# Splitting the value products of two attentions into one sum, and moving the first raw MLP weights

## The chip, the cores and the metric

The kernel runs on one core of one Trainium2 chip. A core has several engines that work side by side, each through its own instructions in order: TensorE (PE) multiplies matrices, with its weight loads shown apart as PEld; VectorE (DVE) and ScalarE (ACT) do elementwise work and read what TensorE left in PSUM; GpSimd (POOL) does some elementwise work; SyncE (SP) issues most of the DMA transfers. Data lies in HBM, in SBUF (128 partitions) and in PSUM, where matmuls accumulate. Engines wait for one another through semaphores.

The metric is the device time of one execution in microseconds (us). The kernel before took 1761.11 us, the median of three runs (1760.59 to 1767.72).

## What is computed

One layer of a decoder trunk on 1024 tokens of width 1024, in float32:

```python
h = rms_norm(x, pre_mix_g[l])
proj = h @ w_in[l]
...
oa = diff_attention(qa, ka, va, lam)
oa = rms_norm(oa, diff_head_g[l]) * (1.0 - lam_init)
ya = oa.reshape(b, s, A_WIDTH) @ w_a_out[l]
...
for g, (window, dil) in enumerate(B_PAIRS):
    o_g, lse_g = dilated_group(qb[:, :, g], kb[:, :, g], vb[:, :, g], window, dil)
...
yb = ob.reshape(b, s, B_WIDTH) @ w_b_out[l]
g_a, g_b = jnp.split(jax.nn.sigmoid(gates), 2, axis=-1)
mix = (g_a * ya + g_b * yb) @ w_mix_out[l]
x = x + rms_norm(mix, post_mix_g[l])
h = rms_norm(x, pre_ffn_g[l])
u = causal_depthwise_conv(h @ w_up[l], conv_w[l], conv_b[l])
gate, val = jnp.split(u, 2, axis=-1)
y = (jax.nn.gelu(gate, approximate=True) * val) @ w_down[l]
x = x + rms_norm(y, post_ffn_g[l])
```

Attention A has 4 heads with two score maps each (softmax one minus lambda times softmax two, then times the values). Attention B has three groups of 4 heads, each a band of a strided subsequence. In both, the last step is a product of probabilities and values, and that step is one of the two places of the change. The other is the loading of `w_up`, the first weights of the MLP.

## The kernel before

**Split operands.** A float32 number is kept as two tiles of a type that TensorE multiplies fast, `hi` and `lo`: ACT copies the number into `hi` (L143) and VectorE subtracts that from it into `lo` (L140). This is `split`. A full product is three matmuls, hi x hi, hi x lo and lo x hi, that accumulate in one PSUM bank (`mm3`, L147 to L149).

**Stages, in order.** Projections and attention A, with projections of the next heads and of gates as filling between attention steps; attention B, filled the same way (about 80 to 925 us); branch A (`ya`) and branch B, each a product with an output matrix, times a gate; the mixing product row by row (`mix_row`, L989 to L991) with two normalizations and transposes (L980); the MLP in 22 blocks of 128 columns per half; the down product. Within the MLP the first three blocks (`full`) take 16 x 3 matmuls per unit; the others (`seven`) use a scheme with seven products of half size instead of eight, on sums of weights (`weights`) and sums of activations (t1 to t4).

**Value products.** `turned` transposes a block of probabilities on TensorE and splits it, so that a block `t` holds hi and lo side by side. `pv` multiplies the value block `vh` (the stationary operand) by hi and lo of `t` in one matmul (L484), into two separate sums that lie side by side in one bank, and `vl` by the hi part alone (L486) into the first sum. A use with two query blocks has 512 columns in L484 and 256 in L486, a use with one has 256 and 128. At the end of a group ACT copies the first sum into `osb` (L580 in attention A, L771 in B), and VectorE adds the second sum to it (L581, L772). The pool `ps_o` of these sums has one buffer.

**Branch B and its memory.** `ob`, the split operands of branch B, is a pool `mid_b` on the left side of SBUF, closed when branch B is issued. For each half of each of its 8 rows VectorE multiplies by the gate (L959), POOL adds `ya` (L960), and `split` writes `mh` and `ml`, which the mixing product reads. Weights of the mixing product are loaded and split in between. The pool `res` is opened after this on the left side, where `mid_b` was: it holds rows of `x`, normalized rows and gains.

**Raw weights.** `load_raw` (L120) loads half a weight unit (256 KB) by SyncE into the pool on top of the list `raws_in`. From branch B on this is `raw`, with five buffers, shared by the weights of branch B, of the mixing product and of the MLP. `slot_w` gives a pair of tiles for hi and lo from `wpool`, six buffers each. The two units of MLP block 0 are made by `up`, started as `first_ups` between the last mixing rows.

**From full to seven-product blocks.** `weights(f)` loads four raw halves a11, a12, a21, a22, splits a11 into `wpool` and a12 into `wb` and so on in turn, and makes the sums s1 to s4 (L1144). For the first such block this is called after the pools `wb` and `mid` have been opened in the memory of the sums t1 to t4, and after the last splits of these (the list `pieces`).

**Order.** The program is written in stages, but the order of the instructions on each engine is set when the program is built, by a planner that simulates a timeline; `tc.high_priority` moves some of them ahead. So an edit in one stage can change the order elsewhere.

Of the kernel before, what the change touches and what calls it, by code (L numbers as in the profile page):

```python
# [24 lines left out]
P = 128  # L25
# [18 lines left out]
FULL = 3  # L44
# [44 lines left out]
def trunk(ctx: ExitStack, tc: tile.TileContext, a, out):  # L89
# [18 lines left out]
    def psum(dt=F32, pool=acc, tag="acc"):  # L108
        return pool.tile([P, 512], dt, tag=tag, name=tag)
# [64 lines left out]
    def halves():  # L174
        return [slice(i * 512, (i + 1) * 512) for i in range(2)]
# [302 lines left out]
    def pv(o, vs, uses, hh, first, last):  # L478

        c = slice(hh * P, (hh + 1) * P)
        for n, (b, q0, q1, t) in enumerate(uses):
            nc.tensor.matmul(o[:, :, q0 : q1 + 1], vs[b // 4][0][:, b % 4, c], t, start=first and n == 0, stop=False)  # L484
        for n, (b, q0, q1, t) in enumerate(reversed(uses), 1):
            nc.tensor.matmul(o[:, 0, q0 : q1 + 1], vs[b // 4][1][:, b % 4, c], t[:, 0], start=False,  # L486
                             stop=last and n == len(uses))


# [30 lines left out]
    def attend_a(h, i, ops, vs, out_sb, pair):  # L520

        q0, q1, k0, k1, l0, l1 = ops
        scale = QK ** -0.5
        if i // 4 not in out_sb:
            out_sb[i // 4] = (wk_a.tile([P, 512], F32, tag="osb", name="osb", bufs=2),
                              tiny.tile([P, 4], F32, tag="eps4", name="eps4", bufs=2))
        osb, eps4 = out_sb[i // 4]
        qs = slice(i * P, (i + 1) * P)
        w = (i + 1) * P
        chunks = [(c, min(w, c + 512)) for c in range(0, w, 512)]  # L530
        mx = tiny.tile([P, 2, 2], F32, tag="mx", name="mx")
        sc = []
        for c, (qq, kk, ll) in enumerate(((q0, k0, l0), (q1, k1, l1))):
            s_sb = wk_a.tile([P, S], F32, tag="s", name="s", bufs=4)
            sc.append(s_sb)
            for n, (c0, c1) in enumerate(chunks):
                ps = psum(F32, ps_s, "s")[:, : c1 - c0]
                nc.tensor.matmul(ps, qq[:, qs], kk[:, c0:c1], start=True, stop=False)
                nc.tensor.matmul(ps, qq[:, qs], ll[:, c0:c1], start=False, stop=True)
                mask = mask_a[:, 512 - (c1 - c0) :] if c1 == w else mask_a[:, 0:1].to_broadcast([P, 512])  # L540
                nc.vector.tensor_tensor_reduce(
                    out=s_sb[:, c0:c1], in0=ps, in1=mask, scale=1.0, scalar=-3.0e38,
                    op0=ALU.add, op1=ALU.max, accum_out=mx[:, c, n : n + 1])
        if len(chunks) == 2:
            nc.vector.tensor_tensor(mx[:, :, 0], mx[:, :, 0], mx[:, :, 1], op=ALU.max)
        negm = tiny.tile([P, 2], F32, tag="negm", name="negm")
        nc.vector.tensor_scalar(negm, mx[:, :, 0], -scale, None, op0=ALU.mult)
        den = tiny.tile([P, 2], F32, tag="den", name="den")
        for c in range(2):
            nc.scalar.activation(sc[c][:, :w], sc[c][:, :w], AF.Exp, bias=negm[:, c : c + 1], scale=scale,  # L550
                                 accum_out=den[:, c : c + 1])
        rc = tiny.tile([P, 1], F32, tag="rc", name="rc")
        nc.vector.reciprocal(rc, den[:, 1:2])
        ratio = tiny.tile([P, 1], F32, tag="ratio", name="ratio")
        nc.vector.scalar_tensor_tensor(ratio, rc, den[:, 0:1], nlam, op0=ALU.mult, op1=ALU.mult)
        nc.vector.scalar_tensor_tensor(sc[0][:, :w], sc[1][:, :w], ratio, sc[0][:, :w], op0=ALU.mult, op1=ALU.add)

        nc.vector.scalar_tensor_tensor(eps4[:, i % 4 : i % 4 + 1], den[:, 0:1], EPS, den[:, 0:1], op0=ALU.mult, op1=ALU.mult)

        pair.append(sc[0])  # L560
        if i % 2 == 0:
            return
        two, po, ts = list(pair), [], {}
        pair.clear()
        groups = [[(b, n) for b in (2 * g, 2 * g + 1) for n in range(2) if b < i or n] for g in range((i + 1) // 2)]

        def turn(g):
            t = turned([two[n][:, b * P : (b + 1) * P] for b, n in groups[g]], wk_a, 3)
            for b in {b for b, _ in groups[g]}:
                at = [x for x, (bb, _) in enumerate(groups[g]) if bb == b]  # L570
                ts[b] = t[:, :, at[0] : at[-1] + 1]

        def add(b):
            if b == 0:
                po.append(psum(F32, ps_o, "o").rearrange("p (t n q) -> p t n q", n=2, t=2))
            uses = [(b, 0, 1, ts[b])] + ([(i, 1, 1, ts[i])] if b == i - 1 else [])
            pv(po[0], vs, uses, h % 2, b == 0, b == i - 1)
            if b == i - 1:
                o = osb[:, (i % 4 - 1) * P : (i % 4 + 1) * P].rearrange("p (n q) -> p n q", n=2)
                nc.scalar.activation(o, po[0][:, 0], AF.Copy)  # L580
                nc.vector.tensor_tensor(o, po[0][:, 1], o, op=ALU.add)  # L581
                if i % 4 == 1:
                    head_norm(h, i // 4, osb, eps4)

        def do(*todo):
            def fn():
                for f, x in todo:
                    f(x)
            return fn

        n = len(groups)
        later(1, do(*[(turn, g) for g in range(min(n, 2))]))
        if n > 2:
# [117 lines left out]
    def attend_b(g, h, jj, ops, vs, sbs):  # L711
# [46 lines left out]
                n += len(bs)  # L758

        def values():  # L760
            po = psum(F32, ps_o, "o").rearrange("p (t j q) -> p t j q", j=2, t=2)
            for us in [uses] if shared else [[us] for us in uses]:
                pv(po, vs, us, h % 2, True, True)
            hi, lo = po[:, 0], po[:, 1]
            if g == 0:
                to = osb[:, 2 * jj * P : 2 * (jj + 1) * P].rearrange("d (j q) -> d j q", j=2)
            elif g == 1:
                to = osb.rearrange("d (j q r) -> d r j q", r=4, j=2)[:, jj]
            else:
                to = osb.rearrange("d (i r) -> d r i", r=8)[:, 2 * jj : 2 * jj + 2]  # L770
            nc.scalar.activation(to, hi, AF.Copy)  # L771
            nc.vector.tensor_tensor(to, lo, to, op=ALU.add)  # L772
            if jj == 3:
                store_b(g, h, osb, stat)

# [173 lines left out]
    with st2:  # L949
# [88 lines left out]
        def up(f, part):  # L1038
# [3 lines left out]
            for half, sl in enumerate(halves()):  # L1042
# [4 lines left out]
                nc.scalar.activation(uu[:, 2 + half * 512 : 2 + (half + 1) * 512], ps, AF.Copy)  # L1047
                yield uu

        first_ups = [up(0, part) for part in range(2)]  # L1050
        for g in first_ups:
            next(g)
            turn_h2.pop(0)()
        assert not turn_h2


# [54 lines left out]
        return to  # L1111

    cv = open_pool(st_up, "cv", side="right")
    with ExitStack() as st_s:
        sums = open_pool(st_s, "sums")
        full(0)
        new_sum("t1", b12, b11)
        new_sum("t3", b22, b12, nc.gpsimd)
        full(1)
        new_sum("t2", b22, tt["t1"])  # L1120
        new_sum("t4", b21, tt["t2"])
        t3, t2, t4 = (split_sum(n) for n in ("t3", "t2", "t4"))
        for f in range(2, FULL):
            full(f)

        t1 = split_sum("t1", b12)
        while pieces:
            pieces.pop(0)()
# [1 line left out]
    wb = open_pool(st_up, "wb")  # L1130
    mid = open_pool(st_up, "mid")

    def weights(f):

        a11, a12, a21, a22 = (load_raw(a["w_up"][2 * f + part][:, sl]) for part in range(2) for sl in halves())
        ws = {}

        def put(name, src):
            ws[name] = slot_w(wb if len(ws) % 2 else None)
            split(*ws[name], src)  # L1140

        def combined(name, x, y, op):
            t = mid.tile([P, 512], F32, tag="s", name=name, bufs=4)
            nc.vector.tensor_tensor(t, x, y, op=op)  # L1144
            return t

        put("a11", a11)
        put("a12", a12)
        s1 = combined("s1", a21, a22, ALU.add)
        s2 = combined("s2", s1, a11, ALU.subtract)  # L1150
        put("s2", s2)
        put("s3", combined("s3", a11, a21, ALU.subtract))
        put("s1", s1)
        put("s4", combined("s4", a12, s2, ALU.subtract))
        put("a22", a22)
        return ws
# [47 lines left out]
            split(*operands[step][-1], src)  # L1204

    places = iter([lambda: slot_w(early, 2), slot_w] * 2 + [slot_w] * 4)
    ws = weights(FULL)
    for f in range(FULL, NF):
        if f + 1 == NF:
            for i in range(AHEAD):  # L1210
# [258 lines left out]
```

## Time and profile before

| what | us |
|---|---|
| median of three runs | 1761.11 |
| the profiled execution's own time | 1762.05 |
| span of its trace, first to last instruction | 1760.3 |

The profile is of one execution. In its rows an instruction group has a line, an engine, an operation and the tiles (`out<-in`); a wait has the engine that waits and the one that released it. Matmuls overlap in TensorE's pipeline, so the duration of one is longer than the distance to the next. The clock column is the share of full speed that TensorE was granted.

### The profile page before, as it was taken

Reading aid. Unit: us, or ns where it says so; the run is one execution under the profiler, and the core shown is the slowest. Engines: PE = TensorE matmul, PEld = TensorE weight load, DVE = VectorE, ACT = ScalarE, POOL = GpSimd, SP = SyncE. Lnnn points to the kernel's source line nnn. Section 1 sums busy time; section 2 is a strip of 40 time slices with the busy share of each in tenths; the row PEclk is TensorE's granted clock in tenths of the full one; section 3 lists DMA queues with packets and bytes.
Section 4 is the critical chain, followed back from the end, with each engine's and each line's share of the span. In section 5 each row is a group of like instructions: output and inputs, shape, how many; then the busy total and the mean of one; then the engine's idle time right before and its main releaser. Section 6 shows DMA issues by size and latency. Waiting matters only on the chain.

```text
span 1760.3 us, 24112 instructions
## 1 busy us (share of the span) xinstructions
PE 1717.8 (98%) x8754; PEld 1455.4 (83%) x8754; DVE 1327.4 (75%) x2612; ACT 867.7 (49%) x1585; POOL 51.6 (3%) x78
## 2 busy tenths in 40 slices
PE   9999999999999999999998999999999999999997
PEld 7887888889888888898777778878888888888886
DVE  4767878776565666565665867799999999689978
ACT  6446565543565644565652523364443444355452
POOL 1000000000000000000000410300000000000000
PEclk9999999999999999999999999999999999999999
DMA  8510112211131334121476532123222222196624
GB/s 275 171 61 25 66 55 78 85 43 55 61 97 55 97 115 145 67 96 55 130 263 207 170 122 106 37 72 108 90 79 96 79 78 100 58 337 218 208 78 156
DMA packets 100407, 197.61 MB, mean 112 GB/s; under 512 B 16368, under 2 KB 23216, under 8 KB 100288
## 3 DMA queue, kind: packets, MB, share of 16 engines
q1 hardware_dynamic: 92192, 185.06, 31.5%
q10 hardware_dynamic: 8096, 11.01, 1.8%
q8 instruction: 68, 1.11, 0.3%
q14 instruction: 51, 0.42, 0.1%
HBM read 152.37 MB, written 43.66 MB: 111 GB/s over the span
## 4 chain that ended last, share of the span: by engine, by line
PE 74%; DVE 10%; DMA 8%; ACT 4%; issue 3%; SPq 0%; POOL 0%; DVEq 0%; ACTq 0%
PE acc L147 14%; PE acc L148 14%; PE acc L149 14%; PE acc L438 3%; PE acc L439 3%; PE acc L440 3%; PE acc L1302 3%; PE acc L1300 3%; PE acc L1301 3%; PE acc L990 2%; PE acc L991 2%; PE acc L989 2%; PE o L484 2%; PE pt L472 1%; DVE wlo L140 1%
## 5 line engine op out<-in xcount | busy, mean ns | idle before, releaser
L147 PE MATMUL acc<-xh,whi 128*128 128x512 f32 x744 | 297.0, 400 | 6.1 <-DVE t L421 3.8
L148 PE MATMUL acc<-xh,wlo 128*128 128x512 f32 x744 | 296.5, 399 | 1.4 <-DVE wlo L140 1.4
L149 PE MATMUL acc<-xl,whi 128*128 128x512 f32 x744 | 294.6, 398 | 0.0
L143 ACT ACTIVATE whi<-raw 128x512 fp32r<-128x512 f32 (+1 forms) x258 | 158.7, 624 | 210.5 <-PE acc L149 127.0
L140 DVE TENSOR_TENSOR wlo<-raw,whi 128x512 fp32r<-128x512 f32 (+1 forms) x255 | 184.8, 731 | 49.0 <-ACT whi L143 47.9
L147 PEld LDWEIGHTS acc<-xh,whi 128*128 128x128 f32 x744 | 140.6, 189 | 36.1 <-DVE t L421 4.4
L148 PEld LDWEIGHTS acc<-xh,wlo 128*128 128x128 f32 x744 | 141.0, 190 | 29.3 <-DVE wlo L140 1.6
L149 PEld LDWEIGHTS acc<-xl,whi 128*128 128x128 f32 x744 | 141.0, 190 | 28.2
L147 PE MATMUL acc<-mh,whi 128*128 128x512 f32 x400 | 155.8, 390 | 1.7 <-ACT whi L143 1.5
L148 PE MATMUL acc<-mh,wlo 128*128 128x512 f32 x400 | 155.7, 389 | 0.2 <-DVE wlo L140 0.2
L149 PE MATMUL acc<-ml,whi 128*128 128x512 f32 x400 | 155.4, 389 | 0.0
L438 PE MATMUL acc<-whi,xh 128*128 128x256 f32 x512 | 147.5, 288 | 1.0 <-DVE t L421 1.0
L440 PE MATMUL acc<-wlo,xh 128*128 128x256 f32 x512 | 146.9, 287 | 0.0
L439 PE MATMUL acc<-whi,xl 128*128 128x256 f32 x512 | 146.8, 287 | 0.0
L420 ACT ACTIVATE t<-acc 64x512 f32<-64x512 f32 (+1 forms) x160 | 94.7, 592 | 41.5 <-PE acc L149 37.9
L1175 DVE TENSOR_TENSOR u<-acc,u 128x512 f32<-128x512 f32 x133 | 90.6, 685 | 25.6 <-PE acc L149 25.5
L438 PEld LDWEIGHTS acc<-whi,xh 128*128 128x128 f32 x512 | 97.7, 191 | 2.2 <-DVE t L421 1.4
L143 ACT ACTIVATE whi<-s 128x512 fp32r<-128x512 f32 x76 | 47.2, 627 | 106.0 <-PE acc L149 94.5
L439 PEld LDWEIGHTS acc<-whi,xl 128*128 128x128 f32 x512 | 97.7, 191 | 0.7
L440 PEld LDWEIGHTS acc<-wlo,xh 128*128 128x128 f32 x512 | 97.7, 191 | 0.1
L147 PEld LDWEIGHTS acc<-mh,whi 128*128 128x128 f32 x400 | 75.1, 188 | 17.9 <-ACT whi L143 1.9
L148 PEld LDWEIGHTS acc<-mh,wlo 128*128 128x128 f32 x400 | 75.1, 188 | 16.0 <-DVE wlo L140 0.5
(313 smaller groups left out, 3859.6 us busy)
## 6 DMA issues: line engine op xcount, KB each, us to landing
raw<-in_w_in SPq DMA_DIRECT2D x126, 256.0 KB, 2.6
raw<-in_w_up SPq DMA_DIRECT2D x88, 256.0 KB, 2.7
raw<-c_d SPq DMA_DIRECT2D x48, 256.0 KB, 3.3
c_d<-c SPq DMA_DIRECT2D x22, 512.0 KB, 2.7
raw<-in_w_down SPq DMA_DIRECT2D x37, 256.0 KB, 3.6
gl<-gt_d SPq DMA_DIRECT2D x16, 512.0 KB, 6.0
gt_d<-gate ACTq DMA_DIRECT2D x26, 256.0 KB, 2.2
og_d<-osb SPq DMA_DIRECT2D x12, 512.0 KB, 4.3
```

The costliest lines, as they stand in the source:

```text
L140: eng.tensor_tensor(lo, src, hi.bitcast(F32), op=ALU.subtract)
L143: nc.scalar.activation(hi, src, AF.Copy)
L147: nc.tensor.matmul(o, sh, mh, start=first, stop=False)
L148: nc.tensor.matmul(o, sl, mh, start=False, stop=False)
L149: nc.tensor.matmul(o, sh, ml, start=False, stop=last)
L420: nc.scalar.activation(t1[dst], ps[src], AF.Copy)
L438: nc.tensor.matmul(ps, xh[:, k, tk], wh[:, w], start=k == 0, stop=False)
L439: nc.tensor.matmul(ps, xl[:, k, tk], wh[:, w], start=False, stop=False)
L440: nc.tensor.matmul(ps, xh[:, k, tk], wl[:, w], start=False, stop=k == KC - 1)
L1175: nc.vector.tensor_tensor(to, made(p), x, op=ALU.add)
L1300: nc.tensor.matmul(banks[m], gh[:, tk], wh, start=f == 0, stop=False)
L1301: nc.tensor.matmul(banks[m], gl[:, tk], wh, start=False, stop=False)
```

## The change

Three edits.

1. `pv` no longer multiplies `vh` by hi and lo in one matmul into two sums. It issues one matmul for each part, and all three products accumulate in the same sum, which has half the columns. After a group ACT's copy is the only evacuation: the adds of L581 and L772 are removed.
2. While `first_ups` is started, `res` is on top of `raws_in`. The four raw halves of MLP block 0 so get a tag of their own in `res` with its default of two buffers, in place of buffers of `raw`.
3. The raw halves a11 and a12 of the first seven-product block are loaded and split before the last sum t1 is split, both into `wpool`; `weights` takes them as given and loads and splits only the rest.

```diff
         for n, (b, q0, q1, t) in enumerate(uses):
-            nc.tensor.matmul(o[:, :, q0 : q1 + 1], vs[b // 4][0][:, b % 4, c], t, start=first and n == 0, stop=False)
+            for part in range(2):
+                nc.tensor.matmul(o[:, q0 : q1 + 1], vs[b // 4][0][:, b % 4, c], t[:, part], start=first and n == part == 0,
+                                 stop=False)
         for n, (b, q0, q1, t) in enumerate(reversed(uses), 1):
-            nc.tensor.matmul(o[:, 0, q0 : q1 + 1], vs[b // 4][1][:, b % 4, c], t[:, 0], start=False,
+            nc.tensor.matmul(o[:, q0 : q1 + 1], vs[b // 4][1][:, b % 4, c], t[:, 0], start=False,
                              stop=last and n == len(uses))
...
-                po.append(psum(F32, ps_o, "o").rearrange("p (t n q) -> p t n q", n=2, t=2))
+                po.append(psum(F32, ps_o, "o")[:, : 2 * P].rearrange("p (n q) -> p n q", n=2))
...
-                nc.scalar.activation(o, po[0][:, 0], AF.Copy)
-                nc.vector.tensor_tensor(o, po[0][:, 1], o, op=ALU.add)
+                nc.scalar.activation(o, po[0], AF.Copy)
...
-            po = psum(F32, ps_o, "o").rearrange("p (t j q) -> p t j q", j=2, t=2)
+            po = psum(F32, ps_o, "o")[:, : 2 * P].rearrange("p (j q) -> p j q", j=2)
...
-            nc.scalar.activation(to, hi, AF.Copy)
-            nc.vector.tensor_tensor(to, lo, to, op=ALU.add)
+            nc.scalar.activation(to, po, AF.Copy)
...
+        raws_in.append(res)
         first_ups = [up(0, part) for part in range(2)]
         for g in first_ups:
             next(g)
             turn_h2.pop(0)()
+        raws_in.pop()
...
+    raw_of_a = {}
...
+        first_ws = {}
+        for i, name in enumerate(("a11", "a12")):
+            raw = raw_of_a[name] = load_raw(a["w_up"][2 * FULL][:, halves()[i]])
+            first_ws[name] = slot_w()
+            split(*first_ws[name], raw)
+
         t1 = split_sum("t1", b12)
...
-    def weights(f):
+    def weights(f, ws=(), a1=()):
...
-        a11, a12, a21, a22 = (load_raw(a["w_up"][2 * f + part][:, sl]) for part in range(2) for sl in halves())
-        ws = {}
+        a11, a12 = a1 or (load_raw(a["w_up"][2 * f][:, sl]) for sl in halves())
+        a21, a22 = (load_raw(a["w_up"][2 * f + 1][:, sl]) for sl in halves())
+        ws = dict(ws)

         def put(name, src):
-            ws[name] = slot_w(wb if len(ws) % 2 else None)
-            split(*ws[name], src)
+            if name not in ws:
+                ws[name] = slot_w(wb if len(ws) % 2 else None)
+                split(*ws[name], src)
...
-    ws = weights(FULL)
+    ws = weights(FULL, first_ws, raw_of_a.values())
```

More of the change, by code (lines that the diff above doesn't have):

```diff
@@ L760, in values @@
         def values():
-            po = psum(F32, ps_o, "o").rearrange("p (t j q) -> p t j q", j=2, t=2)
+            po = psum(F32, ps_o, "o")[:, : 2 * P].rearrange("p (j q) -> p j q", j=2)
             for us in [uses] if shared else [[us] for us in uses]:
                 pv(po, vs, us, h % 2, True, True)
-            hi, lo = po[:, 0], po[:, 1]
             if g == 0:
```

## The prediction

> **What bounds the kernel now.** I read the page first, then the table of busy time by stretch, then the waits of TensorE, and last the timelines around its longest gaps.
>
> ```profile
> PE 1717.8 (98%) x8754; PEld 1455.4 (83%) x8754; DVE 1327.4 (75%) x2612; ACT 867.7 (49%) x1585; POOL 51.6 (3%) x78
> ```
>
> TensorE (PE) is busy for 98% of the span; no other engine comes near. So the time is about TensorE's own work plus its few gaps, and an edit counts by what it does to those two. Two stretches that the change touches (columns: length, then busy us and instructions of PE, PEld, DVE, ACT and POOL, then granted clock, DMA share, GB/s):
>
> ```profile
> 80.00:925.00 845.00, 828.29 (x4835) 723.25 (x4833) 567.21 (x1413) 467.78 (x948) 1.59 (x4) 0.99 0.26 86
> ...
> 1128.00:1190.00 62.00, 59.89 (x262) 48.72 (x262) 61.43 (x59) 33.46 (x51) 9.17 (x10) 1.00 0.18 60
> ```
>
> From 80 to 925 us lie the two attentions, with projections as filling. TensorE is at 828 of 845 us there and VectorE (DVE) only at 567: matmul time is what costs, and VectorE has room. From 1128 to 1190 us, where the MLP changes from its full blocks to its seven-product blocks, it is VectorE that never rests (61.43 of 62). TensorE's waits in the attentions (us in total, times, longest):
>
> ```profile
> PE o L484 <- DVE pt L140: 4.3, 3, 2.1
> ...
> PE s L147 <- DVE bmx L736: 0.4, 1, 0.4
> ```
>
> These are the first and the last of ten such rows, which add up to 16.2 us. None of the ten names the add of L581 or L772, which the change deletes.
>
> **Part A: products of probabilities and values.** The tile view of the sums `o`:
>
> ```profile
> L484 PE MATMUL o<-pt,vh x188: 277/389/582, 140.7 to 918.2; 128*128 128x512 f32 x96, 128*128 128x256 f32 x92
> ...
> L486 PE MATMUL o<-pt,vl x188: 218/278/366, 141.0 to 918.3; 128*128 128x256 f32 x96, 128*128 128x128 f32 x92
> ...
> L772 DVE TENSOR_TENSOR osb<-o,osb x48: 411/618/720, 462.1 to 922.9; 128x256 f32<-128x256 f32 x48
> ...
> L581 DVE TENSOR_TENSOR osb<-o,osb x16: 417/420/425, 152.6 to 427.8; 128x256 f32<-128x256 f32 x16
> ```
>
> Each L484 instruction becomes two with half the columns: 96 of 512 columns become 192 of 256, and 92 of 256 become 184 of 128. So TensorE gets 188 matmuls more, with the same number of columns in all. L486 stays. The adds go: 48 x 0.618 + 16 x 0.420 = 36 us of VectorE by the medians.
>
> A matmul's shown duration contains its pipeline, so what it costs is read from the distance between starts. In the chain of waits (start, length, name), and in the timelines of TensorE and of its weight loads:
>
> ```profile
> 1050.21 0.87 PE pt L980 x8
> ...
> 1569.88 0.91 PE acc L1300 x4
> ```
>
> ```profile
> 467.07 0.28 PE L440 MATMUL acc<-wlo,xh 128*128 128x256 f32 x1
> 467.19 0.28 PE L438 MATMUL acc<-whi,xh 128*128 128x256 f32 x1
> ```
>
> ```profile
> 904.38 0.19 PEld L486 LDWEIGHTS o<-pt,vl 128*128 128x128 f32 x1
> ...
> 904.83 0.19 PEld L148 LDWEIGHTS acc<-xh,wlo 128*128 128x128 f32 x1
> ```
>
> Four matmuls of 512 columns take 0.91 us, 0.227 each. One of 256 takes 0.12. Eight of 128 (transposes) take 0.87, 0.109 each, nearly as much as 256 columns. The last pair shows why: over four loads, those of two matmuls of 128 columns (L486) and two of 256 or more, the starts move by 0.45 us, 0.113 each. Below about 256 columns it is the weight load that sets the pace. Would the second half need a load, as its weights are those of the first? L538 and L539 already are such a pair (both take the same block of queries as weights):
>
> ```profile
> L538 PEld LDWEIGHTS s<-k,q 128*128 128x128 f32 x96 | 18.1, 189 | 3.6 <-DVE mx L541 1.3
> L539 PEld LDWEIGHTS s<-l,q 128*128 128x128 f32 x96 | 18.1, 189 | 2.2
> ```
>
> Both load, 96 times each. So a split of 256 columns costs 2 x 0.113 - 0.12 = 0.106 us, times 92 = 9.8 us; a split of 512 costs 2 x 0.12 - 0.227 = 0.013, times 96 = 1.2. **Added on TensorE: 11 us**, all on the path, as it is at 98% there. Bounds: 0 if columns alone counted (0.227 / 4 for 128), 11.6 if each of the 92 cost a full 0.113 more.
>
> The Trainium skill, "TensorE: Matmul & The Clock Gate", section "Back-to-back issue gap", gives about 81 ns for a sustained pair of weight load and matmul of 128 columns; by that, as an estimate, two would take 0.162 us, and 92 splits of 0.12 us would add 3.9. The trace's 0.109 to 0.113 disagrees and decides here. Its section "Step-by-step: what each phase is for" says that one can load once and matmul repeatedly; the rows of L538 and L539 show that this program doesn't.
>
> What comes back: ACT's copy now ends a group, `o` is free 0.4 to 0.6 us earlier, and VectorE's queue is 36 us shorter over 845. Of the 16.2 us of waits, 14.0 are for VectorE and 2.2 for ACT, but none for the deleted adds; only the queue gets shorter, by a fifteenth of its work (36 of 567). Bounds 0 and -16; nearest to the fifteenth (1 us), with an allowance as each shortened stall may also save a lowered clock: **-3 us**. Below zero it could go too: the order on all engines is planned anew, and a stall of the present size (2.1) can appear.
>
> **Part B1: raw weights of the first MLP block.** Their four loads (two halves of two units) no longer go into the five-buffer pool `raw` but into two buffers of `res`, whose memory held `ob`, the operands of branch B. So they can't be issued before branch B's last matmul. VectorE, then ACT, then TensorE around the end of branch B:
>
> ```profile
> 1006.05 1.64 DVE L140 TENSOR_TENSOR wlo<-raw,whi 128x512 fp32r<-128x512 f32 x1 [0.27 <-ACT whi L143]
> ...
> 1009.42 0.68 DVE L959 TENSOR_TENSOR gl<-acc,gl 128x512 f32<-128x512 f32 x1
> ```
>
> ```profile
> 1010.33 0.63 ACT L143 ACTIVATE whi<-raw 128x512 fp32r<-128x512 f32 x1 [2.53 <-DMA raw<-in_w_up]
> 1011.99 0.63 ACT L143 ACTIVATE whi<-raw 128x512 fp32r<-128x512 f32 x1 [1.02 <-DMA raw<-in_w_up]
> 1012.53 0.61 ACT L143 ACTIVATE mh<-gl 128x512 fp32r<-128x512 f32 x1
> ```
>
> ```profile
> 1013.19 0.78 PE L989 MATMUL acc<-whi,mh 128*128 128x512 f32 x1 [2.30 <-ACT mh L143]
> 1015.30 0.80 PE L990 MATMUL acc<-whi,ml 128*128 128x512 f32 x1 [1.33 <-DVE ml L140]
> ```
>
> ```profile
> 1012.00:1024.00 12.00, 9.48 (x30) 7.29 (x31) 10.31 (x13) 5.11 (x9) 4.87 (x3) 0.72 0.82 287
> ```
>
> The mixing matmuls wait for `mh` and `ml`, and ahead of these in both queues stand splits of `w_up`: 1.64 us of VectorE at 1006, and two ACT splits that wait for their loads (2.53 and 1.02) with `mh` of 1012.53 behind them. TensorE loses 2.30 + 1.33 us, and its clock falls (0.72 over 12 us is 3.4 us of clock, part of it while it stands): up to 7.0 us in all. If the four loads come only after branch B, the splits at 1006 go, L959 moves up by about 1.9 us, near to the 2.30 wanted. What is late next is `mh` of the last block, one step behind it. Not all goes: the new loads land (2.5 us after issue, by the wait above) around 1010, with the last blocks still in work, and the second block's loads can take the freed `raw` buffers. Bounds 0 and -7.0; I take **-5**, nearer the full end since the clock goes with the gap. The moved splits have cover: the first MLP matmuls come after the mixing rows, whose transposes (L980, above) begin near 1050. On SyncE the gains and the rows of `x` stand behind the waiting loads; they are wanted only when the first mixing row is normalized, and the cost is nothing unless that cover of some 20 us is used up.
>
> The same page of the Trainium skill, section "What's actually happening", has the clock fall after an idle window of about 3.4 us; by that a gap of 2.30 would cost no clock, and as an estimate the bound would be 3.6, not 7.0. The 0.72 of this stretch disagrees.
>
> **Part B2: a11 and a12 of the first seven-product block** are loaded and split ahead of the splits of t1, both into `wpool`.
>
> ```profile
> 1176.55 0.39 PE L149 MATMUL acc<-ml,whi 128*128 128x512 f32 x1
> 1178.43 0.50 PE L147 MATMUL acc<-mh,whi 128*128 128x512 f32 x1 [1.49 <-ACT whi L143]
> ...
> 1181.98 0.39 PE L147 MATMUL acc<-mh,whi 128*128 128x512 f32 x1
> 1182.76 0.50 PE L148 MATMUL acc<-t2h,wlo 128*128 128x512 f32 x1 [0.39 <-DVE wlo L140]
> ```
>
> Against a step of 0.227, 1.65 and 0.55 us are lost, 2.2 in all. With a11 and a12 ready, products p1 and p2 (24 x 0.227 = 5.4 us) run from 1176.8 to 1182.2. Late next are the splits of the sums, which VectorE, full, delivers no earlier than now (before 1182.76): about 0.5 stays. **-1.7 us**; bounds 0 and -2.2, and +1 if the moved splits push the sums back. The loads are no cost: DMA is at 0.18 in this stretch.
>
> **The sum.** +11 - 3 - 5 - 1.7 = +1.3 us. The profiled execution took 1762.05 us, so 1763.4; it lies 0.9 above the median of the runs, 1761.11, and against that I say **1762.4**.
>
> **Rivals.** (1) *The added matmuls cost nothing*: columns set the pace, or the second half's load is hidden. For: the column count is unchanged. Against: 0.109 for 128 columns, and L539's loads. 1762.4 - 11 = 1751.4. The sentence "load once and matmul repeatedly" above is its rule. Chance 0.08. (2) *VectorE's relief is worth more*: shorter queues end most of the waits on it, -10 instead of -3, and B1 its full -7. For: 14.0 of the 16.2 us are waits for VectorE. Against: they wait for its work of other kinds. 1753.4. Chance 0.20. (3) *Slower: the stall before the mixing rows stays.* The loads, issued at branch B's end (1006.7), land near 1009.5, and an ACT split that waits for them is again placed ahead of `mh` (1012.53 now). It decides if that split stands before that `mh` in ACT's order; then B1 is 0 and A's relief, at most 1, leaves 1761.11 + 11 - 1 - 1.7 = 1769.4, and with one more lowered clock (3.4) 1772.8. For: ACT's order has this now. Against: the loads are tied to a later event. Chance 0.20. (4) *The change doesn't do what it says*: the memory of `res` is free no later than `raw` is, the early splits stay where they are, and only A and B2 act: 1761.11 + 11 - 3 - 1.7 = 1767.4. Chance 0.07.
>
> **How the numbers follow.** The forecast has the rest, 0.45, within about 5 us either way. The range reaches from 1751, where (1) lies, to 1772, most of (3). About 0.5% (8.8 us) is what a measurement of this kernel can tell from no change: below 1752.3 counts as faster, above 1769.9 as slower. Faster: (1), and a third of (2): 0.15. Slower: two thirds of (3) and the forecast's edge: 0.18. Within: 0.67.
>
> **What would show it.** A: 188 more matmuls, TensorE's time from 80 to 925 us longer by about 11 less what its waits lose, VectorE's shorter by 36. B1: no `w_up` split before 1006, and a clock of 1.0 where 0.72 stood. B2: no wait for `whi` at the first seven-product block. Wrong would be: 128-column starts 0.06 us apart in L484, or a new gap where the planner has put a split ahead of `mh`.

## The result and the profile after

| | before | after |
|---|---|---|
| median of five runs each, us | 1761.11 (1759.64 to 1767.72) | 1752.02 (1749.53 to 1754.48) |
| profiled execution: own time, span, us | 1762.05, 1760.3 | 1754.33, 1752.5 |

The ratio is 0.9943, with a 95% interval of 0.9921 to 0.9965: 9.1 us less by the medians. The forecast was no change that can be told, 1762.4, in a range from 1751 to 1772. The range just holds the time; the sign of the sum is wrong.

Where the time went is read by three marks in TensorE's instructions: the first product of branch B (tile `obh`), the last mixing matmul (L991 before, L990 after) and the end of the span. The rows of the two tile and line views, before and then after (count, shortest, median and longest duration in ns, first and last start in us):

```profile
L147 PE MATMUL acc<-obh,whi x64: 388/389/389, 942.9 to 1006.0; 128*128 128x512 f32 x64
...
L991 PE MATMUL acc<-wlo,mh x128: 388/389/628, 1007.1 to 1105.6; 128*128 128x512 f32 x128
```

```profile
L147 PE MATMUL acc<-obh,whi x64: 389/389/389, 940.3 to 1001.5; 128*128 128x512 f32 x64
...
L990 PE MATMUL acc<-wlo,mh x128: 387/389/476, 1002.6 to 1096.4; 128*128 128x512 f32 x128
```

| stretch | before | after | difference | the prediction had |
|---|---|---|---|---|
| start to first `obh` (part A) | 942.9 | 940.3 | -2.6 | +11 - 3 = +8 |
| first `obh` to last mixing matmul (B1) | 162.7 | 156.1 | -6.6 | -5 |
| from there to the end (B2) | 654.7 | 656.1 | +1.4 | -1.7 |
| span | 1760.3 | 1752.5 | -7.8 | +1.3 |

So nearly all of the error lies in the first stretch, and there it isn't the price of the matmuls. The page's engine line, then the stretches whose rows of before the prediction shows:

```profile
PE 1724.8 (98%) x8942; PEld 1469.5 (84%) x8942; DVE 1295.2 (74%) x2548; ACT 868.1 (50%) x1585; POOL 50.5 (3%) x78
```

```profile
80.00:925.00 845.00, 838.25 (x5038) 739.66 (x5037) 540.39 (x1356) 473.14 (x953) 1.62 (x4) 1.00 0.28 89
...
1128.00:1190.00 62.00, 60.47 (x258) 49.13 (x257) 61.93 (x72) 33.56 (x52) 2.84 (x9) 0.97 0.23 77
1012.00:1024.00 12.00, 12.00 (x55) 9.93 (x54) 6.07 (x10) 4.07 (x7) 0.00 (x0) 1.00 0.52 187
```

The page counts 188 matmuls more (8942 against 8754). In the attentions TensorE is busy for 838 us of 845, where it was for 828: ten us more of work stand where gaps were. The stretch at 1012 has no gap and a clock of 1.00, where it had 9.48 us of 12 and 0.72. At the change to the seven-product blocks VectorE is as full as before (61.93 of 62), and the clock is 0.97 where it was 1.00.

All waits of TensorE from 80 to 925 us after the change (what waits, for what; us in total, times, longest):

```profile
PE acc L148 <- DVE wlo L140: 1.5, 1, 1.5
PE o L613 <- ACT sq L605: 1.0, 1, 1.0
PE acc L438 <- DVE t L421: 1.0, 1, 1.0
PE o L485 <- DVE pt L140: 0.9, 1, 0.9
PE acc L147 <- DVE t L421: 0.9, 1, 0.9
PE pt L621 <- DVE spread L616: 0.6, 1, 0.6
PE s L540 <- DVE mx L543: 0.4, 1, 0.4
PE pt L472 <- ACT bs L744: 0.4, 1, 0.4
```

They add up to 6.7 us, against 16.2. The wait of the value products for their split probabilities (`pt`), 4.3 us in three before, is one of 0.9. The waits for VectorE fell from 14.0 to 5.3, though VectorE's work in this stretch fell only from 567 to 540.

**Was the price of the matmuls right?** The groups by shape of the split product up to 940 us (count, busy us and mean ns of one, idle before), and the weight loads of one group in the timeline (start, length, count):

```profile
L485 PE MATMUL o<-pt,vh 128*128 128x256 f32 x192 | 46.3, 288 | 0.0
L485 PE MATMUL o<-pt,vh 128*128 128x128 f32 x184 | 35.0, 243 | 0.9 <-DVE pt L140 0.9
```

```profile
L485 PEld LDWEIGHTS o<-pt,vh 128*128 128x128 f32 x376 | 64.1, 190 | 4.6 <-DVE pt L140 1.1
```

```profile
906.97 0.42 PEld L485 LDWEIGHTS o<-pt,vh 128*128 128x128 f32 x2
907.31 0.19 PEld L488 LDWEIGHTS o<-pt,vl 128*128 128x128 f32 x1
907.42 0.30 PEld L485 LDWEIGHTS o<-pt,vh 128*128 128x128 f32 x2
907.65 0.19 PEld L488 LDWEIGHTS o<-pt,vl 128*128 128x128 f32 x1
907.76 0.19 PEld L148 LDWEIGHTS acc<-xh,wlo 128*128 128x128 f32 x1
```

192 and 184 matmuls, as counted in advance, and all 376 load their weights. The loads of six 128-column matmuls (two, one, two and one) go by with no other between; from 907.42 to 907.76 three of them take 0.34 us, 0.113 each. Whoever looks for 0.06 doesn't find it. To count over the whole stretch I fitted a pace per matmul to start distances in undisturbed runs of the trace: 0.2285 us for 512 columns, 0.178 for 384, 0.1197 for 256, 0.1135 for 128, 0.114 for the 64 of one column, 0.1095 for a transpose. Times the counts ahead of the first `obh` (before: 2616, 32, 1898, 280, 64 and 344 transposes; after: 2520, 32, 1998, 464, 64 and 344) this is 907.4 us before and 918.3 after: **+10.9**, the +11 of the sum. The pace of 128 columns is the least sure of them: the few runs of this trace with 128-column matmuls alone give 0.105, and with that the sum is +9.3. What is left up to the first `obh`, counted from the first matmul at 1.2 us, I call *gaps* below: 942.9 - 1.2 - 907.4 = 34.3 before, 20.8 after. They shrank by 13.5 us. Gaps so counted also hold what a lowered clock costs, but in this difference the clock has no part: the record of the granted clock has 10.2 us at half speed ahead of the first `obh` in both traces.

### The profile page after: what moved, and what is told of

Read it like the earlier page. It is cut to its first block, busy times and chain, and to the rows that moved or that the text cites. A ratio compares the mean times of both kernels' runs of the same rounds, so it can differ in the third digit from the quotient of the medians.

```text
span 1752.5 us, 24382 instructions
## 1 busy us (share of the span) xinstructions
PE 1724.8 (98%) x8942; PEld 1469.5 (84%) x8942; DVE 1295.2 (74%) x2548; ACT 868.1 (50%) x1585; POOL 50.5 (3%) x78
## 4 chain that ended last, share of the span: by engine, by line
PE 77%; DVE 8%; DMA 8%; ACT 3%; issue 3%; SPq 1%; POOL 0%; DVEq 0%; ACTq 0%; POOLq 0%
PE acc L147 15%; PE acc L148 15%; PE acc L149 15%; PE acc L438 3%; PE acc L440 3%; PE acc L439 3%; PE acc L1312 2%; PE acc L1313 2%; PE acc L1311 2%; PE o L485 2%; PE pt L472 2%; PE acc L989 2%; PE acc L990 2%; PE acc L988 2%; DVE wlo L140 1%
## 5 line engine op out<-in xcount | busy, mean ns | idle before, releaser
L140 DVE TENSOR_TENSOR wlo<-raw,whi 128x512 fp32r<-128x512 f32 (+1 forms) x255 | 180.5, 716 | 57.2 <-ACT whi L143 56.4
L147 PEld LDWEIGHTS acc<-xh,whi 128*128 128x128 f32 x744 | 140.5, 189 | 34.5 <-ACT xh L342 3.7
L149 PEld LDWEIGHTS acc<-ml,whi 128*128 128x128 f32 x400 | 75.1, 188 | 15.7
```

Source lines behind the costliest of these rows:

```text
L140: eng.tensor_tensor(lo, src, hi.bitcast(F32), op=ALU.subtract)
L147: nc.tensor.matmul(o, sh, mh, start=first, stop=False)
L149: nc.tensor.matmul(o, sh, ml, start=False, stop=last)
```

## The experiments

"Ratio" is that of the median to runs of the kernel before on the same chip, with its 95% interval; 0.001 is 1.76 us. Three readings of the missing 11 us are compared. *Relief*: the deleted adds are worth far more than -3. *Order*: the planner found a better order by luck. *Absorption*, which came up only with the result of `e4_split_keep`: the added TensorE work costs less than its 11, since it fills gaps.

### The parts alone

Each of the three edits of the diff by itself (`e1_products`: edit 1; `e2_res`: edit 2; `e3_a11`: edit 3).

> The value products alone. By the lengths of the stages in the trace of the changed kernel the two attentions are 2.6 us shorter, so both theories expect about 1758.5 us (-2.6), with about 11 us more of matmul pace from the first scores to the first matmul of branch B and some 13.7 us less of gaps there. The prediction's term of -3 for the gaps would give 1769.

> The raw weights of MLP block 0 in res, alone. Prediction: -5 us. By the stage lengths of the changed kernel (branch B and mixing rows 162.7 to 156.1 us): -6.6, so about 1754.5, with no stretch of half clock near 1013 us. If those gaps fell because the stage was entered in another state (other planning upstream) and not by the edit: 0.

> a11 and a12 ahead of the splits of t1, alone. Prediction: -1.7 us. By the stage lengths of the changed kernel (first up to last t4 430.0 to 431.0 us): 0 to +1, with the wait moved to the low half of a weight sum of t2's product.

| run | median us | ratio | gaps | first `obh` to last mixing | rest |
|---|---|---|---|---|---|
| before | 1759.99 | 1 | 34.3 | 162.7 | 654.7 |
| `e1_products` | 1757.5 | 0.9981 [0.9971, 0.999] | 22.2 | 158.8 | 656.1 |
| `e2_res` | 1756.92 | 0.9987 [0.9978, 0.9996] | 33.5 | 157.7 | 655.3 |
| `e3_a11` | 1762.81 | 1.0015 [1.0005, 1.0024] | 37.2 | 160.8 | 655.0 |

The last three columns are of one profiled execution each; a ratio is of the medians. The products alone close the gaps, 34.3 to 22.2, by a little more than the 10.9 they add, and the whole gains 3.3 us (0.0019 x 1760). The raw weights do their 5.0 us in their own stretch; over all they gain 2.3, where 5 to 6.6 was expected, or nothing if the gaps had fallen for another reason. The early splits of a11 and a12 bring nothing: expected was 0 to +1 us, and alone they cost 2.6 (0.9 to 4.2).

`e3_a11` also shows how far one trace can be trusted. Its list of TensorE's instructions is that of before as far as the MLP's sums of activations, and still its first `obh` starts at 945.8, not 942.9: up to 3 us between two executions, here with 5.1 us more lost to a lowered clock. A gap of one trace is good to about 3 us.

The parts alone sum to 0.9981 - 1 + 0.9987 - 1 + 1.0015 - 1 = -0.0017, 3 us; the whole change gains 8 to 10 (0.9955 below, 0.9943 above). So they seem to work on one another, which the pairs test.

### Pairs

`e6_after` is the whole change again; `e7_products_res` leaves out edit 3, `e8_products_a11` edit 2.

> The whole change, beside the rest on one chip. The three parts alone gave -2.5, -3.1 and +2.8 us, together -2.8. If parts add up: 1757 (ratio 0.998). If they help one another: 1751 to 1752 (0.994 to 0.995), as in the comparison of the two kernels.

> The change without a11 and a12. If parts add up: -5.6, 1754.4. If the a11 part costs what it cost alone (+2.8), this is that much faster than the whole change; if it helps only where the stages before it are shorter, it is slower than the whole change.

> The change without the raw weights in res. If parts add up: +0.3, 1760.3. If the whole change's extra gain lies in the pair of products and a11: 1755.

| run | median us (before: 1761.78) | ratio | gaps | first `obh` to last mixing | rest |
|---|---|---|---|---|---|
| `e6_after` | 1754.19 | 0.9955 [0.9939, 0.9971] | 20.7 | 156.7 | 654.9 |
| `e7_products_res` | 1752.46 | 0.9946 [0.9931, 0.996] | 21.0 | 155.0 | 653.9 |
| `e8_products_a11` | 1758.64 | 0.9982 [0.997, 0.9993] | 21.3 | 161.9 | 655.4 |

Edit 2 behind the products is worth 0.9946 - 0.9981 = -6.2 us, and behind the products and edit 3, from `e8_products_a11` to `e6_after`, 0.9955 - 0.9982 = -4.8 us; alone it was 2.3. Each of these differences is good to about 3 us. Edit 3 costs 0.0009 (1.6 us) between `e7_products_res` and `e6_after`, and 0.0001 between `e1_products` and `e8_products_a11`: nothing that these intervals separate from zero, and no gain. Of the expectations, the gain of the whole is nearer to parts that help one another; `e8_products_a11` lies between its two.

### The products taken apart: the split, the adds

`e4_split_keep` has the 188 matmuls more, but still fills two sums and adds them:

```diff
-            nc.tensor.matmul(o[:, :, q0 : q1 + 1], vs[b // 4][0][:, b % 4, c], t, start=first and n == 0, stop=False)
+            for part in range(2):
+                nc.tensor.matmul(o[:, part, q0 : q1 + 1], vs[b // 4][0][:, b % 4, c], t[:, part],
+                                 start=first and n == part == 0, stop=False)
```

> The matmuls are split as in the change, but the two sums and VectorE's adds stay. Theory 'relief' (the adds' absence is what took the gaps away): only the cost is seen, +11 us, about 1772. Theory 'order' (the gaps fell since the planner laid the attentions out anew, the adds have little to do with it): the gaps fall here too, 1761 to 1766.

`e5_noadds` has the matmuls of before, without the adds:

```diff
-                nc.vector.tensor_tensor(o, po[0][:, 1], o, op=ALU.add)
...
-            nc.vector.tensor_tensor(to, lo, to, op=ALU.add)
```

> VectorE's adds of the low sums are left out (so that part of the value product is left out), with the matmuls of before. Theory 'relief': the gaps in the attentions fall by 8 us or more, 1752 or less. Theory 'order': the gaps change by the luck of the new order, anything within 4 us of before, and not below 1756.

| run | median us (before beside it) | ratio | gaps | first `obh` to last mixing | rest |
|---|---|---|---|---|---|
| `e4_split_keep` | 1760.58 (1759.99) | 1.0002 [0.9993, 1.0012] | 29.7 | 158.3 | 654.5 |
| `e5_noadds` | 1756.88 (1761.78) | 0.9969 [0.9957, 0.9981] | 34.5 | 158.3 | 654.0 |

The page's engine line of `e4_split_keep`, and its stretch from 80 to 925 us:

```profile
PE 1727.2 (98%) x8942; PEld 1471.2 (83%) x8942; DVE 1328.2 (75%) x2612; ACT 867.8 (49%) x1585; POOL 51.5 (3%) x78
```

```profile
80.00:925.00 845.00, 835.16 (x5009) 736.84 (x5008) 563.90 (x1407) 465.52 (x946) 1.59 (x4) 0.99 0.26 85
```

The 188 matmuls are there, the adds too (VectorE's 2612 instructions), and TensorE is busy for 1727.2 us instead of 1717.8. Yet the kernel isn't 11 us slower: +0.4, with an interval from -1.2 to +2.1. The time is neither the 1772 of *relief* nor quite the 1761 to 1766 of *order*. With VectorE's work nearly as before (563.9 against 567.2 us), TensorE's waits from 80 to 925 us add up to 9.5 us instead of 16.2, in seven rows of which this is the first:

```profile
PE o L485 <- DVE pt L140: 2.8, 1, 2.8
```

So some 7 of the 11 us seem to have gone into waits. The gaps fell by only 4.6, as this trace has 17.1 us at half speed ahead of the first `obh`, where before has 10.2. The stretch after them is 4.4 shorter, and of that 3.4 is clock too: before has 6.8 us at half speed there, this trace none. The traced execution took 1763.78 us, 3.2 above the median, so the cost of 0.4 rests on the medians, and the 7 us on one trace.

Without the adds, but also without the split, the waits of TensorE from 80 to 925 us begin with this row:

```profile
PE o L484 <- DVE pt L140: 5.3, 3, 2.7
```

The gaps are as large as before (34.5), the value products even wait 5.3 us for `pt` instead of 4.3, and the 5 us gained lie later. In this order the relief alone does nothing in the attentions, as *order* expected, and the split alone 5 us; the two together 12. That can't be told from luck with one order. It needed others.

### The same in other orders

The planner moves some instructions ahead by an offset of 30. I changed it to 24 and to 40, at its four places, which changes the order of instructions and nothing else:

```diff
-    with tc.high_priority(offset=30):
+    with tc.high_priority(offset=40):
```

In each order ran the kernel before, the products, the split with the adds kept, and the adds left out with the matmuls of before.

> The kernel before with another order and the same work: the priority offset of the attention steps is 24 in place of 30. Theory 'order': the start of branch B (942.9 us in the trace of before) moves by several us, and the difference to the products kernel with the same offset may have either sign. Theory 'edit': whatever the order, the kernel with the products of the change is 1 to 5 us ahead there.

> The value products alone with the offset 24. Theory 'edit': its branch B starts 1 to 5 us earlier than that of before with 24. Theory 'order': anywhere from 10 us earlier to 10 us later.

> The kernel before with the offset 40: the same two expectations, compared with the products kernel at 40.

> The value products alone with the offset 40. Theory 'edit': branch B starts 1 to 5 us earlier than in before with 40. Theory 'order': anywhere from 10 us earlier to 10 us later.

> Split matmuls with both sums and the adds kept, offset 24. Gaps are the time to the first matmul of branch B less the pace of its matmuls (before 35 us in the mean of five traces, with the products 22 in six). Theory 'absorbed' (longer TensorE work fills gaps by itself): gaps near 22 to 26 here too, and the whole time within 4 us of before with 24 (1759.0). Theory 'both' (split and absent adds are both needed): gaps 28 to 35, time 1762 to 1770.

> The same with offset 40, against before with 40 (1757.8 us, gaps 37.4 us). Absorbed: gaps near 22 to 26, time within 4 us of 1757.8. Both needed: gaps 30 to 37, time 1761 to 1769.

> The adds left out (and with them the low part of the value product), the matmuls of before, offset 24. If the absent adds alone take gaps away: gaps 19 to 27, time 1759.0 - 8 = 1751 or less. If both are needed, or if the longer TensorE work absorbs gaps: gaps stay at 30 to 37, time 1754 to 1760.

> The adds left out (and with them the low part of the value product), the matmuls of before, offset 40, against before with 40 (1757.8 us, gaps 37.4 us). If the absent adds alone take gaps away: gaps 24 or less, time 1749 or less. Otherwise gaps 32 to 40, time 1753 to 1759.

Ratios to the kernel before at offset 30, and in parentheses the gaps ahead of the first `obh` in the trace:

| offset | neither | split alone | adds gone alone | both (the products) |
|---|---|---|---|---|
| 30 | 1 (34.3) | 1.0002 (29.7) | 0.9969 (34.5) | 0.9981 (22.2) |
| 24 | 0.9983 [0.9974, 0.9992] (32.2) | 1.0006 [0.9997, 1.0016] (32.4) | 0.9927 [0.9911, 0.9944] (21.8) | 0.9943 [0.9927, 0.9959] (26.4) |
| 40 | 0.9972 [0.9961, 0.9983] (37.3) | 0.9967 [0.9954, 0.998] (26.9) | 0.9885 [0.9863, 0.9907] (27.3) | 0.9926 [0.9911, 0.9941] (22.2) |

The medians behind it are 1759.0, 1761.63, 1748.27 and 1753.0 us at 24, and 1757.81, 1754.49, 1742.54 and 1749.19 at 40. Read along the rows (a difference of two ratios is good to 0.001 to 0.003):

- The split alone: +0.0002, +0.0023, -0.0005. With the adds gone: +0.0012, +0.0016, +0.0041. On average 1.2 and 4.0 us, not 11.
- The adds gone: -0.0031, -0.0056, -0.0087. With the split: -0.0021, -0.0063, -0.0041. On average -10.2 and -7.3 us, not -3.
- Both: -0.0019, -0.0040, -0.0046: -3.3, -7.0 and -8.1 us, in all three orders faster.

In the order of the change itself, 30, the adds are worth 5.5 us without the split and 3.7 with it.

So *order* does not do as the whole explanation: leaving the adds out gains in all six comparisons, each by more than the interval of the difference, though three orders are few and each kernel still has an order of its own. Order does set how much, 3.3 to 8.1 us for the products, and where it shows. At 24 the adds alone take the gaps from 32.2 to 21.8, which at 30 they leave as they are. TensorE's waits from 80 to 925 us, summed over the rows of each trace, are 16.2, 9.5, 16.8 and 7.7 us at 30 (neither, split, no adds, both), 15.0, 14.2, 10.2 and 7.1 at 24, 14.5, 11.0, 10.0 and 8.8 at 40. What one part alone takes away depends on the order; both together leave 7 to 9 us in each.

At 24 and at 40 the kernel before also waits for the deleted add by name, which it did not at 30. The rows of its waits at 24, then at 40:

```profile
PE o L484 <- DVE osb L772: 1.7, 2, 1.4
```

```profile
PE o L484 <- DVE osb L772: 4.2, 3, 2.2
```

There the next value product waits until VectorE has read the one buffer `o`, so part of the relief in these orders is the buffer that comes free earlier.

Not all expectations held. At 24 the products start branch B not 1 to 5 us earlier but 5.0 later (945.9 against 940.9); their gain there lies behind it, in the stretch to the last mixing matmul (152.6 us against 160.5). At 40 they start it 1.4 earlier. The split alone at 24 has the gaps of "both needed" (32.4) and starts branch B 11 us later than before at 24 (951.9): in the attentions of this trace the full price is paid, and nothing is absorbed. Its time is still within 4 us by the medians, 1761.63 against 1759.0, where the traced execution took 1766.0. At 40 the split agrees with "absorbed", but for gaps 0.9 above the range. The adds left out agree with "alone" at 24 and, by the time, at 40, where the gaps (27.3) lie between the two expectations.

The stretch from 80 to 925 us at offset 40, of the kernel before and then with the adds left out:

```profile
80.00:925.00 845.00, 830.26 (x4847) 725.97 (x4846) 568.89 (x1416) 469.48 (x952) 1.59 (x4) 0.99 0.27 88
```

```profile
80.00:925.00 845.00, 834.68 (x4878) 729.25 (x4877) 545.31 (x1364) 473.80 (x955) 1.62 (x4) 1.00 0.27 89
```

TensorE has the matmul forms of before and is busy for 834.7 us of 845 instead of 830.3: 31 matmuls more fit into the same stretch.

### The raw weights where no gap is left

Edit 2 at offset 40, without and with the products:

> The raw weights of MLP block 0 in res alone, offset 40. With the old offset this gave -2.3 us by itself and -6.2 behind the products. If the edit is worth its stage's 5 us in any order: 1757.8 - 5 = 1753. If its worth depends on the order in which the stage is entered: anything from 1751 to 1760; with the old products at 40 there is no gap before the first mixing row (60.0 us for branch B), so 2 to 3 us at most.

> Products and res, offset 40: the version expected to be fastest. Products alone at 40 took 1749.2 us and have no more than 1 us of gaps in branch B and the mixing rows, so res can give 1 us there: 1748 to 1750. If res were worth 6 us wherever it stands: 1743.

`p_res_40` took 1751.8 us, a ratio of 0.994 [0.9921, 0.9959]; `p_products_res_40` 1749.24, 0.9924 [0.9905, 0.9943]. Against their kernels without edit 2 (0.9972 and 0.9926) that is -5.6 us and -0.4. TensorE's waits from 925 to 1110 us at offset 40, of the kernel before and then of the products, say why:

```profile
PE acc L147 <- DVE ya L927: 3.3, 2, 3.1
PE acc L989 <- ACT mh L143: 1.7, 1, 1.7
PE acc L990 <- DVE ml L140: 1.6, 1, 1.6
```

```profile
PE acc L147 <- DVE ya L926: 1.8, 3, 0.9
PE acc L990 <- DVE wlo L140: 0.4, 1, 0.4
PE pt L979 <- DVE hn L1025: 0.4, 1, 0.4
PE acc L147 <- ACT mh L143: 0.2, 1, 0.2
```

In the first the waits of the mixing matmuls (L989, L990) for `mh` and `ml` are there to win back, 3.3 us, and a lowered clock beside them (0.86 from 1012 to 1024 us); against the expectation, which saw no gap there, `p_res_40` has won both. In the second no mixing matmul waits for them. `p_products_40` and `p_products_res_40` are the fastest of the kernels here that compute the whole layer, about 3 us below the change's own runs.

## Why the prediction failed, step by step

**+11 for the matmuls: the price was right, the bill was not.** 10.9 us by the counts and paces. The step that failed is the half sentence "all on the path, as it is at 98% there". 98% of 845 us left 17 us of idle time, more than the 11 that were added, and a gap in which TensorE waits for VectorE can close from both sides: when the awaited work comes sooner, or when TensorE has more of its own to do first. `e4_split_keep` measures it: 188 matmuls for 0.4 us, with 7 us less of waits in the attentions. In the two other orders they cost 4.1 and -0.9 us. That they fill waits is seen in the traces at 30 and, less, at 40 (14.5 to 11.0 us), but not at 24; why the whole kernel lost only 4.1 us there, though its attentions grew by 11 in the trace, stays open. Rival (1) had the added matmuls cost nothing for another reason, that columns set the pace; its reason falls with the 376 loads, though its time, 1751.4, is close. By the same rows the sentence "load once and matmul repeatedly" of the Trainium skill ("TensorE: Matmul & The Clock Gate", "Step-by-step: what each phase is for") stays something this program does not do.

**-3 for VectorE's relief: too small; -3.7 to -5.5 in the change's own order, -7 to -10 in the mean of three.** The deleted adds were 34.0 us of VectorE by their busy time (27.3 for L772, 6.7 for L581), not 36. I took the queue to be shorter "by a fifteenth of its work" and the waits to shrink in that ratio. But a wait is the small difference between two engines' long sums of work, so I now expect it to shrink by microseconds, not in the ratio of the sums; that is an argument, which no run isolates. Measured is that with 27 us less work on VectorE from 80 to 925, and ten more on TensorE, 8.7 of the 14.0 us of waits for VectorE are gone. That no wait named a deleted add misled me: it was so in one order only, and there the waits named other work of the same queue. Rival (2) was the nearest: it had -10 for the relief and came to 1753.4. It, too, put all 11 on the path, and its nearness is partly luck: its +1 for part A is 3.6 more than the trace's -2.6, and its -1.7 for B2 is 3.1 less than the +1.4. How the relief divides into the shorter queue and the sum `o` that comes free earlier is not separated: leaving the adds out does both, and only at 24 and 40 do the waits name the second.

**-5 for B1: the mechanism was right; the size depends on the order and on the clock.** TensorE around the end of branch B after the change:

```profile
1006.02 0.39 PE L990 MATMUL acc<-wlo,mh 128*128 128x512 f32 x1
1007.21 0.50 PE L988 MATMUL acc<-whi,mh 128*128 128x512 f32 x1 [0.80 <-ACT mh L143]
1008.32 0.50 PE L989 MATMUL acc<-whi,ml 128*128 128x512 f32 x1 [0.62 <-DVE ml L140]
```

The waits of 2.30 and 1.33 are 0.80 and 0.62, at the same two tiles, and the clock stays up. What is late next is `mh`, as forecast. ACT in these microseconds:

```profile
1002.42 0.63 ACT L143 ACTIVATE mh<-gl 128x512 fp32r<-128x512 f32 x1 [1.17 <-POOL gl L959]
1006.52 0.63 ACT L143 ACTIVATE mh<-gl 128x512 fp32r<-128x512 f32 x1 [3.47 <-POOL gl L959]
```

No split stands between the two; ACT waits for POOL's sum with `ya` (L959 now). In `e1_products`, with the products but without edit 2, TensorE waits there nearly as long as before (3.1 us against 3.6), so these waits don't go with the adds:

```profile
PE acc L989 <- DVE ml L140: 1.7, 1, 1.7
PE acc L988 <- ACT mh L143: 1.4, 1, 1.4
```

The stretch gave -5.0 alone and -6.6 in the whole change, but not all of the -6.6 is edit 2's: with the products alone it is 158.8 us, 3.9 less than before. Of the fall from before, 3.4 us is clock (6.8 us at half speed in this stretch, none after), and the clock does not always fall with these waits, which the forecast took for granted: `e1_products` has 3.4 us at half speed there, and `e4_split_keep` none, though its TensorE is busy for only 8.57 of the 12 us from 1012. Rivals (3) and (4) fall: no weight split is ahead of the late `mh`. What the forecast didn't say is that the term is worth the gap it finds: -5.6 at offset 40, -0.4 there behind the products. Its "2.5 us after issue" was read from ACT's idle time; the page's median from issue to landing is 2.7, which changes nothing.

**-1.7 for B2: failed; no gain.** TensorE at the first seven-product block after the change:

```profile
1170.08 0.39 PE L149 MATMUL acc<-ml,whi 128*128 128x512 f32 x1
1170.66 0.50 PE L147 MATMUL acc<-t2h,whi 128*128 128x512 f32 x1 [0.20 <-ACT whi L143]
1171.18 0.50 PE L147 MATMUL acc<-mh,whi 128*128 128x512 f32 x1
1173.00 0.50 PE L148 MATMUL acc<-t2h,wlo 128*128 128x512 f32 x1 [1.32 <-DVE wlo L140]
1173.34 0.40 PE L149 MATMUL acc<-t2l,whi 128*128 128x512 f32 x1
...
1173.89 0.63 PE L148 MATMUL acc<-t2h,wlo 128*128 128x512 f32 x1
1174.31 0.63 PE L149 MATMUL acc<-t2l,whi 128*128 128x512 f32 x1
```

The wait for a11 (1.49) is gone (0.20), as the step said. But TensorE doesn't run 24 products in the time won, as I assumed: after one of them its order has a product of the sum `t2h`, and its low weights come from VectorE, which hardly rests here (61.93 of 62). The wait moved by one tile, from ACT's `whi` to VectorE's `wlo`, and its size stayed: 0.20 + 1.32 against 1.49. The error is that of taking the order of before for that of after. `e7_products_res`, without edit 3, has the old wait. All waits of TensorE from 1160 us to the end:

```profile
PE acc L147 <- ACT whi L143: 1.5, 1, 1.5
PE acc L148 <- DVE wlo L140: 0.6, 2, 0.4
```

In the whole change they are these:

```profile
PE acc L148 <- DVE wlo L140: 1.3, 1, 1.3
PE pt L1311 <- ACT whi L143: 0.4, 1, 0.4
PE acc L1312 <- DVE wlo L140: 0.4, 1, 0.4
PE acc L147 <- ACT whi L143: 0.2, 1, 0.2
```

2.1 us without edit 3, 2.3 with it. The 2.6 us that `e3_a11` lost by its runs aren't found in the last stretch of its trace (655.0 against 654.7), so where they lie is open.

**The sum.** With measured values in its terms, in the profiled execution: -2.6 - 6.6 + 1.4 = -7.8. Against the +1.3 of the forecast that is 9.1 less: 10.6 less in part A, 1.6 less in B1, 3.1 more in B2. The +1.4 is less sure than its decimals: `e6_after`, the same kernel, has 654.9 for that stretch, 1.2 less, and the 3.4 us at half speed at 1173.7 us, which neither `e6_after` nor before has, can cost 1.7. `e1_products` and `e2_res`, without edit 3, have such a piece too, at 1175.3 and 1173.9 us, so it needn't be edit 3's doing. The chances were as far off as the terms: 0.15 stood on faster by over 0.5%, and the measured 0.57% (0.35 to 0.79) lies just beyond that bound. That a measurement tells only 0.5% from no change was too coarse: this one is good to 0.22%.

## What to carry to other kernels

On an engine at 98%, work that is added is not simply on the path: compare it with the idle time of that stretch, and ask whether the gaps are waits for another engine, which added work can fill; whether it does depends on the order. Size the relief of a helper engine by its whole microseconds against the waits on that engine, not by its share of the queue, and count what stands behind a deleted instruction, not only who waits for it by name. And where a planner sets the order, repeat a comparison in two or three orders that differ by a neutral knob: here that knob alone moved the time by 0.2 to 0.3%, as much as the parts that were being measured.

## What the hardware showed that I had not expected

- Half speed comes in pieces of 3.4 us, mostly one, sometimes two together, in the clock record of each of these traces (and for the last 8 to 11 us of each), and the same instructions do not always get them: ahead of branch B there are 10.2 us of it before and 20.5 in `e3_a11`, whose TensorE instructions are the same up to there. In the rows of the seven-product block above, the starts at 1173.89 and 1174.31 are 0.42 us apart instead of 0.227. The 10 us there, after the change:

```profile
1171.00:1181.00 10.00, 8.66 (x30) 6.67 (x30) 10.00 (x15) 3.49 (x8) 0.10 (x1) 0.83 0.45 159
```

  The Trainium skill ("TensorE: Matmul & The Clock Gate", "What's actually happening") has the clock fall after an idle window of about 3.4 us. Here 0.20 and 1.32 us of waits within 2.4 us were followed by it, so this trace doesn't bear that length out. Nor is a wait enough: from 1012 to 1024 us in `e4_split_keep` TensorE stands for 3.4 of 12 us, and the clock is 1.00.
- A 128-column matmul of this type takes 0.1135 us, one of 256 columns 0.1197, one of a single column 0.114: below 256 columns, width is nearly free.
- Two executions with the same TensorE instructions up to branch B reached it 2.9 us apart (942.9 and 945.8). Differences of that size in one trace carry no argument without the runs beside them.
